# Sums by token behind further products in two attention layers, more rows ahead of the first logits, and a last bank in two halves

## The chip, the cores and the metric

The kernel runs on one core of a Trainium2 chip. The metric is the device time of one execution in microseconds (us). TensorE (PE) multiplies, VectorE (DVE), ScalarE (ACT) and GpSimd (POOL) do the elementwise work, SyncE (SP) issues the transfers; each of them works through its own list of instructions in order, and they wait for one another by semaphores. TensorE's results land in PSUM, which has eight banks of 512 float32 columns.

## The reference

Two decoder layers over 256 tokens of width 1024, in float32. Each layer is a half-step SwiGLU, a mixer, another half-step SwiGLU and a gated embedding. The mixer of layer 0 is latent attention (MLA), that of layer 1 forgetting attention (FoX). Cut to what matters here:

```python
def rms_norm(x, g):
    xf = x.astype(jnp.float32)
    y = xf * lax.rsqrt(jnp.mean(xf * xf, axis=-1, keepdims=True) + EPS)
    return (y * g.astype(jnp.float32)).astype(x.dtype)

def mla_mixer(hn, pos, w_in, g_q_lat, w_uq, g_kv_lat, w_ukv, g_qn, g_kn, w_o):
    z = hn @ w_in                                  # 512 + 256 + 32 columns
    c_q, c_kv, k_pe = ...
    q = (rms_norm(c_q, g_q_lat) @ w_uq).reshape(b, s, 16, 64 + 32)
    kv = (rms_norm(c_kv, g_kv_lat) @ w_ukv).reshape(b, s, 16, 64 + 64)
    k = jnp.concatenate([k_nope, k_pe_h], axis=-1)
    q, k = rms_norm(q, g_qn), rms_norm(k, g_kn)    # per head, then rope
    o = block_causal_attention(q, k, v)
    return o.reshape(b, s, 1024) @ w_o

def fox_mixer(hn, w_in, b_f, g_qn, g_kn, w_o):
    z = hn @ w_in                                  # q, k, v, and 16 forget logits
    log_f = jax.nn.log_sigmoid(f_logit)
    decay = jnp.cumsum(log_f, axis=1)
    o = block_causal_attention(rms_norm(q, g_qn), rms_norm(k, g_kn), v, decay)
    return o.reshape(b, s, 1024) @ w_o

    # the end of each layer
    gate = jax.nn.sigmoid(rms_norm(h, g_ple[i]) @ ple_w_gate[i])
    h = h + gate * (p[i] @ ple_w_proj[i])
```

## The kernel before

**Products.** Each float32 product is three passes in the rounded format float32r: high part by high part, low weight by high part, high weight by low part (L264 to L266 where the weights stream, `mm_x`; L234 to L236 where the tokens stream, `mm_w`). Weights come in units of up to 1 MB: SyncE loads a unit into one of three `raw` buffers (L70), ScalarE casts it to `whi` (L86), VectorE subtracts to get `wlo` (L87), each in pieces of up to 1024 columns; there are six `whi` and `wlo` buffers. Units are prefetched two ahead, at each `w.get()`. TensorE's results go to two PSUM tiles of two banks each, `pa`, and four of one bank, `pb`.

**Norms.** The RMS norms need sums of squares. ScalarE squares, GpSimd adds up chunks (`sq`, `ss` at L384 and L388; `zq` at L827 and L828), and TensorE sums over the partitions with a column of 1/1024, `mean_d`. `by_token` (L406) gives the mean square of each token with two matmuls of one column; `mean_squares` (L775) does the same for the latents of MLA. These sums are plain float32 matmuls.

**MLA.** `zmm(c)` multiplies by the 256 columns c of `w_in`; `latent(c)` turns them into the two parts of `zt` and their squares `zq`. Columns 2 and 3 are keys and rope, 0 and 1 queries. Then `keys(g)` (12 matmuls of 512 columns) and `queries(g)` (24 of 384) give keys, values and queries of four heads, g from 0 to 3. A head's norm for queries needs the token's mean square of the query latent, which is the sum over `zq` of columns 0 and 1: it stands at the end of `queries(0)`.

**Pairs.** Eight pairs of heads are worked on. `turn` transposes a pair's queries and keys (L612) into `qt` (copied by ScalarE, L616) and `kt` (VectorE, L614); `weigh` makes the logits (L518, L519), VectorE's maximum (L523), ScalarE's exponentials (L534), VectorE's division; `turn_back` transposes the weights (L547) into `pt` (one head by VectorE, one by ScalarE); `mix` multiplies by the values (L559, L564). In `mixed` (L710) the early parts, `keys` and `queries` 0 and 1 in MLA, run first; the late ones are fed between the steps of the pairs by a budget of rows, `each / 4` behind each step, with `each` 4 in MLA and 8 in FoX.

**FoX.** `group(272)` makes four heads of values and the forget logits, then `by_token` gives the norm. `dense(g)` (L1008) makes the queries, then the keys of four heads, each 48 matmuls of 256 columns; `more(g)` makes six heads of values.

**The end.** `ple_last` keeps tokens on the partitions: four products of half the depth by 512 output columns for two token tiles, 12 matmuls each, then a sigmoid from PSUM, a multiplication, an addition and a transfer for each 256 columns (L1134, L349, L1137).

**Order.** `steady`, `order` and `queue` are switches: while one is on, its instructions (matmuls; weight casts and subtractions; loads) keep the order of the program. What is not held may be placed by the scheduler.

Of the kernel before, what the change touches and what calls it, by code (L numbers as in the profile page):

```python
# [151 lines left out]
def trunk(ctx: ExitStack, tc: tile.TileContext, a: dict, out: bass.AP):  # L152
# [209 lines left out]
    class Norm:  # L362
# [38 lines left out]
        def by_token(self):  # L401
# [3 lines left out]
            for tt in range(2):  # L405
                nc.tensor.matmul(  # L406
                    ms[:, tt : tt + 1], lhsT=ss[:, tt * P : (tt + 1) * P], rhs=mean_d[:, 0:1], start=True, stop=True
                )
# [300 lines left out]
    def mixed(early, late, each, ready, pair, o, after):  # L709
# [8 lines left out]
        for j in range(-1, KD + 2):  # L718
# [8 lines left out]
            if 0 <= j < KD:  # L727
# [4 lines left out]
                rows.run(each / 4)  # L732
# [11 lines left out]
    def mla(norm, after, pool):  # L744
# [28 lines left out]
        def mean_squares(ps, zq):  # L773
            for tt in range(2):
                nc.tensor.matmul(  # L775
                    ps[:, tt : tt + 1], lhsT=zq[:, 0, tt * P : (tt + 1) * P], rhs=mean_d[:, :1], start=True, stop=True
                )
# [82 lines left out]
        def keys(g):  # L860
            wt = w.get()
# [24 lines left out]
            if g == 0:  # L886
                head_norms(ms, rk, 1, 2)
                norm_keys(g)

        def queries(g):  # L890
# [32 lines left out]
            got[g] = qn, kn, rk  # L923
            ready.add(g)

        def pair(j):
            qn, kn, rk = got[j // 2]
# [6 lines left out]
    def fox(norm, after, pool):  # L934
# [15 lines left out]

        v = pool.tile([P, 2, HEADS, VD], F32, name="v", tag="v", bufs=1)
# [56 lines left out]
        def dense(g):  # L1008

            ps = pa().rearrange("p (u t c) -> p u t c", u=2, t=2)  # L1010
            for u in range(2):
                wt = w.get()
                for k in range(KD):
                    for tt in range(2):
                        mm_x(ps[:, u, tt, :], wt(k), x, k, tt, start=(k == 0 and tt == 0), stop=(k == KD - 1))
                        yield 3 * PASS
# [267 lines left out]
```

## Time and profile before

| | us |
|---|---|
| median of three runs | 1048.11 |
| lowest, highest | 1047.37, 1049.19 |
| the profiled execution | 1049.13 |
| its span | 1047.4 |
| TensorE busy in it | 1034.1 (99%) |
| VectorE, ScalarE, GpSimd busy | 777.6, 600.0, 77.9 |

The profile is of one execution. A row of a timeline gives the start of an instruction, or of several alike in a row (x4), their time together, the engine, the line of the code, the tiles, and in brackets the engine's idle time before it with what ended it. TensorE's matmuls overlap, so a row's length is more than the distance to the next; the distance between starts is the pace. TensorE's clock was granted at 0.997 of full speed over the whole span.

### The profile page before, as it was taken

What the parts mean: (1) busy time and instruction counts of PE and PEld (TensorE: products, weight loads), DVE (VectorE), ACT (ScalarE), POOL (GpSimd) and SP (SyncE); (2) the same over time, 40 slices, a digit from 0 to 9 for tenths busy, and PEclk for the clock granted to TensorE, in tenths of its full rate; (3) what the DMA queues carried; (4) which work ended last, traced back from release to release, by engine and by line L of the source; (5) the groups of instructions that cost most, each with busy time, mean ns of one, the idle gap of its engine ahead of it and who ended that gap; (6) DMA issues with size and microseconds to landing.
All of it is one profiled execution on the core that took longest, in us unless ns stands there. A gap on an engine that the chain in (4) does not pass through costs nothing.

```text
span 1047.4 us, 16326 instructions
## 1 busy us (share of the span) xinstructions
PE 1034.1 (99%) x6380; PEld 918.5 (88%) x6380; DVE 777.6 (74%) x1369; ACT 600.0 (57%) x903; POOL 77.9 (7%) x99
## 2 busy tenths in 40 slices
PE   8999999999999999999999999999999999999998
PEld 7888888987898888889888888889998988888886
DVE  5888766679979776666987776658888797776664
ACT  6665544568766655455656555535655666554552
POOL 0000000233110000001110000011000200000010
PEclk9999999999999999999999999999999999999999
DMA  7765555524336656556537565554743267555541
GB/s 243 242 226 183 185 181 172 181 93 170 106 107 201 214 188 191 183 185 206 170 126 240 188 201 174 188 154 141 227 135 113 95 197 227 182 185 191 181 161 41
DMA packets 171105, 182.60 MB, mean 174 GB/s; under 512 B 6094, under 2 KB 164372, under 8 KB 171028
## 3 DMA queue, kind: packets, MB, share of 16 engines
q1 hardware_dynamic: 170452, 181.03, 53.7%
q8 instruction: 50, 0.82, 0.3%
q10 hardware_dynamic: 576, 0.53, 0.1%
q14 instruction: 27, 0.22, 0.1%
HBM read 180.50 MB, written 1.05 MB: 173 GB/s over the span
## 4 chain that ended last, share of the span: by engine, by line
PE 94%; DVE 3%; DMA 1%; POOL 1%; ACT 0%; issue 0%; ACTq 0%; DVEq 0%
PE pa L255 46%; PE pa L248 23%; PE pa L264 3%; PE pa L266 3%; PE pa L265 3%; PE pa L234 2%; PE pa L236 2%; PE pa L235 2%; DVE wlo L87 1%; PE pb L612 1%; PE pb L519 1%; PE pb L559 1%; PE pb L547 1%; PE pb L518 1%; DMA xn<-in_x_dram 1%; PE pb L266 1%
## 5 line engine op out<-in xcount | busy, mean ns | idle before, releaser
L87 DVE TENSOR_TENSOR wlo<-raw,whi 128x1024 fp32r<-128x1024 f32 (+2 forms) x351 | 418.5, 1223 | 170.9 <-PE pa L248 71.9
L86 ACT CAST whi<-raw 128x1024 fp32r<-128x1024 f32 (+2 forms) x351 | 351.0, 1016 | 247.0 <-PE pa L255 175.9
L255 PE MATMUL pa<-xa,whi 128*128 128x512 f32 x1408 | 343.9, 395 | 1.9 <-DVE xa L376 1.8
L255 PEld LDWEIGHTS pa<-xa,whi 128*128 128x128 f32 x1408 | 258.7, 189 | 54.1 <-DVE xa L376 3.1
L248 PEld LDWEIGHTS pa<-xa,wlo 128*128 128x128 f32 x1408 | 179.1, 189 | 8.7
L248 PE MATMUL pa<-xa,wlo 128*128 128x256 f32 x1408 | 180.6, 279 | 0.0
L255 PE MATMUL pa<-hid,whi 128*128 128x512 f32 x704 | 169.2, 392 | 0.0
L255 PEld LDWEIGHTS pa<-hid,whi 128*128 128x128 f32 x704 | 128.8, 188 | 25.2
L384 POOL TENSOR_TENSOR sq<-sq 128x512 f32<-128x512 f32 x21 | 37.8, 1800 | 826.9 <-ACT sq L382 813.4
L248 PEld LDWEIGHTS pa<-hid,wlo 128*128 128x128 f32 x704 | 88.3, 188 | 4.0
L248 PE MATMUL pa<-hid,wlo 128*128 128x256 f32 x704 | 89.1, 278 | 0.0
L264 PE MATMUL pa<-whi,xa 128*128 128x256 f32 (+3 forms) x192 | 59.0, 307 | 0.0
L266 PE MATMUL pa<-whi,xa 128*128 128x256 f32 (+3 forms) x192 | 57.6, 300 | 0.0
L265 PE MATMUL pa<-wlo,xa 128*128 128x256 f32 (+3 forms) x192 | 57.2, 298 | 0.0
L234 PE MATMUL pa<-xa,whi 128*128 128x256 f32 x184 | 54.2, 295 | 0.0
L349 DVE TENSOR_TENSOR hid<-hf,hid 128x512 fp32r<-128x512 f32 x44 | 30.4, 692 | 29.0 <-ACT hid L442 29.0
L236 PE MATMUL pa<-xa,wlo 128*128 128x256 f32 x184 | 51.9, 283 | 0.0
L235 PE MATMUL pa<-xa,whi 128*128 128x256 f32 x184 | 51.9, 282 | 0.0
L432 ACT COPY gt<-pa 128x512 f32<-128x512 f32 x44 | 25.8, 586 | 39.1 <-PE pa L248 39.0
L432 ACT COPY hf<-pa 128x512 f32<-128x512 f32 x44 | 25.7, 584 | 28.1 <-PE pa L248 28.1
L438 ACT ACTIVATE gt<-gt 128x512 f32<-128x512 f32 x44 | 27.7, 629 | 19.4 <-DVE gt L349 19.3
L264 PEld LDWEIGHTS pa<-whi,xa 128*128 128x128 f32 x192 | 36.1, 188 | 1.4 <-issue 0.5
(281 smaller groups left out, 1215.1 us busy)
## 6 DMA issues: line engine op xcount, KB each, us to landing
raw<-in_ffn_w_in_dram SPq DMA_DIRECT2D x86, 1024.0 KB, 5.1
raw<-in_ffn_w_out_dram SPq DMA_DIRECT2D x32, 1024.0 KB, 5.2
raw<-in_ffn_w_out_dram SPq DMA_DIRECT2D x16, 768.0 KB, 4.5
raw<-in_ple_w_gate_dram SPq DMA_DIRECT2D x8, 1024.0 KB, 5.8
raw<-in_fox_w_in_dram SPq DMA_DIRECT2D x8, 1024.0 KB, 6.5
raw<-in_mla_w_o_dram SPq DMA_DIRECT2D x4, 1024.0 KB, 5.6
raw<-in_fox_w_o_dram SPq DMA_DIRECT2D x4, 1024.0 KB
raw<-in_mla_w_in_dram SPq DMA_DIRECT2D x3, 1024.0 KB, 6.7
```

Source lines behind the costliest of these rows:

```text
L86: self.order(self.nc.scalar.copy(h, whole))
L87: self.order(self.nc.vector.tensor_tensor(low, whole, h.bitcast(F32), op=ALU.subtract))
L234: steady(nc.tensor.matmul(ps, lhsT=hi, rhs=x[:, k, 0, :], start=start, stop=False, skip_group_check=True))
L235: steady(nc.tensor.matmul(ps, lhsT=hi, rhs=x[:, k, 1, :], start=False, stop=False, skip_group_check=True))
L236: return steady(nc.tensor.matmul(ps, lhsT=lo, rhs=x[:, k, 0, :], start=False, stop=stop, skip_group_check=True))
L248: nc.tensor.matmul(ps[:, 1, :], lhsT=wt(k)[1][:, cols], rhs=x[:, at + k, 0, :], start=False, stop=(k == last), skip_group_check=True,)
L255: nc.tensor.matmul(ps, lhsT=wt(k)[0][:, cols], rhs=x[:, at + k], start=(k == first), stop=False, skip_group_check=True)
L264: steady(nc.tensor.matmul(ps, lhsT=x[:, k, 0, t], rhs=wt[0], start=start, stop=False, skip_group_check=True))
L265: steady(nc.tensor.matmul(ps, lhsT=x[:, k, 0, t], rhs=wt[1], start=False, stop=False, skip_group_check=True))
L266: steady(nc.tensor.matmul(ps, lhsT=x[:, k, 1, t], rhs=wt[0], start=False, stop=stop, skip_group_check=True))
L384: nc.gpsimd.tensor_tensor(sq, sq, self.acc, op=ALU.add)
L432: nc.scalar.copy(o, ps[:, :, 0, :])
```

## The change

**MLA.** `steady` is on from `keys(0)` to the sums for the queries, and `mean_squares` is held by it. The sums move from the end of `queries(0)` to the end of `keys(1)` (`first_queries`), with the norms of the first queries. `zmm(1)` then stands ahead of `keys(0)`, where it stood behind.

**Rows ahead of the first logits.** Behind `turn` of pair 0 `mixed` spends `each` instead of a quarter: three units more in MLA, six in FoX.

**FoX.** `dense(0)` is begun early: its first half, the 48 matmuls of the queries, is issued ahead of `by_token`, which is held there by `steady`.

**End.** In the last 512 output columns the second token tile is two PSUM banks of 256 columns, finished one after the other, in place of one of 512.

```diff
@@ by_token
-                nc.tensor.matmul(
-                    ms[:, tt : tt + 1], lhsT=ss[:, tt * P : (tt + 1) * P], rhs=mean_d[:, 0:1], start=True, stop=True
+                steady(
+                    nc.tensor.matmul(
+                        ms[:, tt : tt + 1], lhsT=ss[:, tt * P : (tt + 1) * P], rhs=mean_d[:, 0:1], start=True, stop=True
+                    )
                 )
@@ mixed
                 pairs.append(pair(j))
                 pairs[j].turn()
-                rows.run(each / 4)
+                rows.run(each / 4 if j else each)
@@ mla (mean_squares is wrapped in steady in the same way)
         def keys(g):
+            if g == 0:
+                steady.on = True
             wt = w.get()
...
             if g == 0:
                 head_norms(ms, rk, 1, 2)
                 norm_keys(g)
+            elif g == 1:
+                first_queries()
+
+        def query_norms(g):
+            kn, ms, rk = got[g][1:4] if g == 0 else got[g]
+            nc.vector.scalar_tensor_tensor(ms[:, 0], ms[:, 0], 1.0 / QK, by_head(yq), op0=ALU.mult, op1=ALU.add)
+            head_norms(ms, rk, 0, 1 if g == 0 else 2)
+
+        def first_queries():
+
+            sq = pb()
+            mean_squares(sq, sqa)
+            steady.on = False
+            nc.vector.scalar_tensor_tensor(yq, sq[:, :2], D / QR, ex, op0=ALU.mult, op1=ALU.add)
+            nc.vector.tensor_scalar(yq, yq, EPS, None, op0=ALU.mult)
+            query_norms(0)
 
         def queries(g):
...
-            if g == 0:
-                sq = pb()
-                mean_squares(sq, sqa)
-                nc.vector.scalar_tensor_tensor(yq, sq[:, :2], D / QR, ex, op0=ALU.mult, op1=ALU.add)
-                nc.vector.tensor_scalar(yq, yq, EPS, None, op0=ALU.mult)
...
-            nc.vector.scalar_tensor_tensor(ms[:, 0], ms[:, 0], 1.0 / QK, by_head(yq), op0=ALU.mult, op1=ALU.add)
-            if g == 0:
-                head_norms(ms, rk, 0, 1)
-            else:
-                head_norms(ms, rk, 0, 2)
+            if g:
+                query_norms(g)
                 norm_keys(g)
@@ fox
-        order.on = True
-        order.on = True
+        order.on = steady.on = True
         Rows(group(272)).all()
         vf = got.pop("ps")
+        zero = dense(0)
+        for _ in range(2 * KD):
+            next(zero)
         xt = norm.by_token()
+        steady.on = False
...
-        mixed([dense(0), more(0), dense(1)], [more(1), dense(2), dense(3)], 8, lambda g: len(got.get(g, ())) == 2, pair, o, after)
+        mixed([zero, more(0), dense(1)], [more(1), dense(2), dense(3)], 8, lambda g: len(got.get(g, ())) == 2, pair, o, after)
@@ ple_last
-        gp = [[both_t[:, tt] for tt in range(2)], [pb() for tt in range(2)]]
+
+        gp = [[(0, both_t[:, 0], 0, 512), (1, both_t[:, 1], 0, 512)], None]
         for kh in range(2):
             for half in range(2):
                 wt = w.get()
-                c = slice(half * 512, (half + 1) * 512)
-                for tt in range(2):
+                if gp[half] is None:
+                    gp[half] = [(tt, pb()[:, : c1 - c0], c0, c1) for tt, c0, c1 in ((0, 0, 512), (1, 0, 256), (1, 256, 512))]
+                for tt, ps, c0, c1 in gp[half]:
                     for k in range(4):
-                        mm_x(gp[half][tt], wt(k), x, kh * 4 + k, tt, start=(kh + k == 0), stop=(kh == 1 and k == 3))
+                        part_of = tuple(z[:, c0:c1] for z in wt(k))
+                        mm_x(ps, part_of, x, kh * 4 + k, tt, start=(kh + k == 0), stop=(kh == 1 and k == 3))
...
-                for tt in range(2):
-                    for q in range(2):
-                        cq = slice(q * 256, (q + 1) * 256)
-                        co = slice(half * 512 + q * 256, half * 512 + q * 256 + 256)
+                for tt, ps, c0, c1 in gp[half]:
+                    for cq in range(0, c1 - c0, 256):
+                        co = slice(half * 512 + c0 + cq, half * 512 + c0 + cq + 256)
...
-                        nc.scalar.activation(gt, gp[half][tt][:, cq], AF.Sigmoid, scale=r[:, tt : tt + 1])
+                        nc.scalar.activation(gt, ps[:, cq : cq + 256], AF.Sigmoid, scale=r[:, tt : tt + 1])
```

How the instructions stand is shown at three places. The rows give the line, the operation, out<-in with the tiles' numbers, and the shape; lines below the first edit have moved up by a few numbers in the code after.

TensorE in MLA, before, around the sums for the queries; `zq_2093` is what GpSimd adds up, the matmuls above them are the last of `queries(0)`, those below the first of `keys(1)`:

```order
L264 MATMUL pa_2262<-whi_2145,zt_1933 128x384
L265 MATMUL pa_2262<-wlo_2146,zt_1933 128x384
L266 MATMUL pa_2262<-whi_2145,zt_1933 128x384
L775 MATMUL pb_2288<-mean_d_118,zq_2093 128x1 x2
L264 MATMUL pa_2321<-whi_2209,zt_1933 128x512
L265 MATMUL pa_2321<-wlo_2210,zt_1933 128x512
L266 MATMUL pa_2321<-whi_2209,zt_1933 128x512
```

The same sums after:

```order
L264 MATMUL pa_2304<-whi_2209,zt_1933 128x512
L265 MATMUL pa_2304<-wlo_2210,zt_1933 128x512
L266 MATMUL pa_2304<-whi_2209,zt_1933 128x512
L778 MATMUL pb_2328<-mean_d_118,zq_2093 128x1 x2
L264 MATMUL pa_2355<-whi_2254,zt_1933 128x384
L265 MATMUL pa_2355<-wlo_2255,zt_1933 128x384
L266 MATMUL pa_2355<-whi_2254,zt_1933 128x384
```

They now have `keys(1)` above and `queries(1)` below them; 48 matmuls of `zmm(1)` that stood between `keys(0)` and `queries(0)` stand ahead of both.

ScalarE in MLA, before, from the casts of the last `uq` unit (`raw_2345`) to the first cast of `w_o` (`raw_2421`), with the exponentials of pair 0 (`sm_2437`, `sm_2450`) and `qt_2466` of pair 1 between:

```order
L86 CAST whi_2493<-raw_2345 128x768
L86 CAST whi_2497<-raw_2345 128x768
L872 ACTIVATE scr_2483<-pa_2427 128x512
L534 ACT_TABLE_LOAD
L534 ACTIVATE sm_2437,mx_2438<-sm_2437,mx_2438,rk_2228 128x128
L534 ACTIVATE sm_2437,mx_2438<-sm_2437,mx_2438,rk_2228 128x256
L534 ACTIVATE sm_2450,mx_2451<-sm_2450,mx_2451,rk_2228 128x128
L534 ACTIVATE sm_2450,mx_2451<-sm_2450,mx_2451,rk_2228 128x256
L616 ACTIVATE qt_2466<-pb_2467,qsc_298 96x512
L878 COPY kn_2480<-pa_2427 128x8x64
L880 ACTIVATE v_2205<-pa_2427,rs_2117 128x256 x2
L86 CAST whi_2614<-raw_2421 128x1024
```

The same stretch after, up to the first two exponentials of pair 0 (`sm_2474`); `raw_2421` is `w_o` again, and `qt_2503` is that of pair 1:

```order
L86 CAST whi_2453<-raw_2345 128x768
L86 CAST whi_2457<-raw_2345 128x768
L878 ACTIVATE scr_2443<-pa_2427 128x512
L86 CAST whi_2581<-raw_2421 128x1024
L618 ACTIVATE qt_2503<-pb_2504,qsc_298 96x512
L884 COPY kn_2440<-pa_2427 128x8x64
L886 ACTIVATE v_2205<-pa_2427,rs_2117 128x256 x2
L536 ACT_TABLE_LOAD
L536 ACTIVATE sm_2474,mx_2475<-sm_2474,mx_2475,rk_2228 128x128
L536 ACTIVATE sm_2474,mx_2475<-sm_2474,mx_2475,rk_2228 128x256
```

The first cast of `w_o` has moved from behind the exponentials of pair 0 to ahead of `qt` of pair 1, and `kn` and `v` of the third group stand ahead of the exponentials.

TensorE at the start of FoX, before, around the sums by token; `ss_6940` is GpSimd's sum, the matmuls above are the last of `group(272)`, those below the first of `dense(0)`:

```order
L264 MATMUL pa_6948<-whi_6900,xa_5326 128x272
L265 MATMUL pa_6948<-wlo_6901,xa_5326 128x272
L266 MATMUL pa_6948<-whi_6900,xa_5326 128x272
L406 MATMUL pb_7017<-mean_d_118,ss_6940 128x1 x2
L264 MATMUL pa_7067<-whi_6951,xa_5326 128x256
L265 MATMUL pa_7067<-wlo_6952,xa_5326 128x256
L266 MATMUL pa_7067<-whi_6951,xa_5326 128x256
```

After:

```order
L264 MATMUL pa_7017<-whi_6955,xa_5326 128x256
L265 MATMUL pa_7017<-wlo_6956,xa_5326 128x256
L266 MATMUL pa_7017<-whi_6955,xa_5326 128x256
L407 MATMUL pb_7076<-mean_d_118,ss_6940 128x1 x2
L264 MATMUL pa_7017<-whi_6985,xa_5326 128x256
L265 MATMUL pa_7017<-wlo_6986,xa_5326 128x256
L266 MATMUL pa_7017<-whi_6985,xa_5326 128x256
```

The sums now stand between the two halves of `dense(0)`, behind the queries (`whi_6955` is the second piece of their weights) and ahead of the keys (`whi_6985`).

At the end of the program the last 12 matmuls are of 256 columns, as the 12 before them, into another bank.

## Rows read from the trace of the kernel before

**Rows 1.** The page, part 1: engine, busy us (share of the span), number of instructions
```profile
PE 1034.1 (99%) x6380; PEld 918.5 (88%) x6380; DVE 777.6 (74%) x1369; ACT 600.0 (57%) x903; POOL 77.9 (7%) x99
```

**Rows 2.** Timeline of TensorE, MLA layer: start us, length us, engine, line, out<-in, [idle <-releaser]
```profile
213.08 0.28 PE L234 MATMUL pa<-xa,whi 128*128 128x256 f32 x1
...
218.74 0.35 PE L264 MATMUL pa<-whi,zt 128*128 128x384 f32 x1
...
220.49 0.45 PE L264 MATMUL pa<-whi,zt 128*128 128x384 f32 x1
...
223.20 0.34 PE L266 MATMUL pa<-whi,zt 128*128 128x384 f32 x1
224.67 0.61 PE L775 MATMUL pb<-mean_d,zq 128*128 128x1 f32 x4 [1.14 <-POOL zq L828]
```

**Rows 3.** Timeline of all engines at the start of the FoX layer
```profile
709.91 5.43 DVE L87 TENSOR_TENSOR wlo<-raw,whi 128x1024 fp32r<-128x1024 f32 x4 [0.97 <-ACT whi L86]
...
710.40 1.59 POOL L388 TENSOR_TENSOR ss<-sq 128x256 f32<-128x256 f32 x1
...
710.60 0.28 PE L266 MATMUL pa<-whi,xa 128*128 128x272 f32 x1
...
712.04 0.61 PE L406 MATMUL pb<-mean_d,ss 128*128 128x1 f32 x4 [1.16 <-POOL ss L388]
```

**Rows 4.** Timeline of VectorE at the end of the program
```profile
1042.83 1.46 DVE L349 TENSOR_TENSOR gn<-gn,xa 128x256 f32<-128x256 f32 x4 [1.34 <-ACT gn L1134]
```

**Rows 5.** Windows: stretch, its us, busy us of each engine (instructions), clock, DMA
```profile
222.50:250.00 27.50, 25.49 (x142) 21.14 (x142) 26.76 (x79) 22.32 (x45) 11.75 (x13) 1.00 0.57 192
```

**Rows 6.** Timeline of TensorE, MLA layer, first logits and transposes
```profile
232.17 0.60 PE L612 MATMUL pb<-ident,qn 128*96 128x128 f32 x4
232.61 0.60 PE L612 MATMUL pb<-ident,kn 128*96 128x128 f32 x4
...
243.06 0.49 PE L518 MATMUL pb<-kt,qt 96*128 96x128 f32 x2 [0.59 <-ACT qt L616]
...
244.47 1.02 PE L547 MATMUL pb<-ident,sm 128*128 128x128 f32 x6
245.70 0.61 PE L612 MATMUL pb<-ident,qn 128*96 128x128 f32 x4 [0.20 <-DVE mx L523]
```

**Rows 7.** Timeline of ScalarE, MLA layer
```profile
220.99 0.60 ACT L770 ACTIVATE zq<-pa 128x512 f32<-128x512 f32 x1 [0.55 <-DVE zt L766]
...
236.82 1.57 ACT L86 CAST whi<-raw 128x768 fp32r<-128x768 f32 x2 [2.37 <-DMA raw<-in_mla_w_uq_dram]
...
238.90 1.28 ACT L534 ACT_TABLE_LOAD   x1
...
242.34 0.67 ACT L616 ACTIVATE qt<-pb,qsc 96x512 f32<-96x512 f32 x1
...
244.09 1.04 ACT L86 CAST whi<-raw 128x1024 fp32r<-128x1024 f32 x1
```

**Rows 8.** Timeline of GpSimd, MLA layer
```profile
221.66 1.29 POOL L827 TENSOR_TENSOR zq<-zq 128x512 f32<-128x512 f32 x1 [2.41 <-ACT zq L770]
223.03 1.59 POOL L828 TENSOR_TENSOR zq<-zq 128x256 f32<-128x256 f32 x1
```

**Rows 9.** Timeline of VectorE, MLA layer
```profile
235.30 1.21 DVE L87 TENSOR_TENSOR wlo<-raw,whi 128x1024 fp32r<-128x1024 f32 x1
...
238.83 0.95 DVE L87 TENSOR_TENSOR wlo<-raw,whi 128x768 fp32r<-128x768 f32 x1
...
239.86 0.68 DVE L614 COPY kt<-pb 96x512 f32<-96x512 f32 x1
...
240.54 0.67 DVE L875 TENSOR_REDUCE msq<-scr 128x8 f32<-128x512 f32 x1
```

**Rows 10.** Timeline of the DMA issues on SyncE, MLA layer
```profile
233.94 8.65 SPq L70 DMA_DIRECT2D raw<-in_mla_w_o_dram  x3
```

**Rows 11.** The page, part 6: DMA issues, count, KB each, median us to landing
```profile
raw<-in_mla_w_o_dram SPq DMA_DIRECT2D x4, 1024.0 KB, 5.6
```

More of the change, by code (lines that the diff above doesn't have):

```diff
@@ L774, in mean_squares @@
             for tt in range(2):
-                nc.tensor.matmul(
-                    ps[:, tt : tt + 1], lhsT=zq[:, 0, tt * P : (tt + 1) * P], rhs=mean_d[:, :1], start=True, stop=True
+                steady(
+                    nc.tensor.matmul(
+                        ps[:, tt : tt + 1], lhsT=zq[:, 0, tt * P : (tt + 1) * P], rhs=mean_d[:, :1], start=True, stop=True
+                    )
                 )
@@ L916, in queries @@
             pool_op(qn[:, :, :, NOPE:], ra, rb, ALU.add)
[L917 to L921 removed]
+            if g:
+                query_norms(g)
                 norm_keys(g)
[L923 removed]
+            got[g] = qn, kn, ms, rk
             ready.add(g)
         def pair(j):
[L927 removed]
+            qn, kn, _, rk = got[j // 2]
             hs = slice(2 * (j % 2), 2 * (j % 2) + 2)
@@ L949, in group, with dense @@
             got["ps"] = ps
+        def dense(g):
+            ps = pa().rearrange("p (u t c) -> p u t c", u=2, t=2)
+            for u in range(2):
+                wt = w.get()
+                for k in range(KD):
+                    for tt in range(2):
+                        mm_x(ps[:, u, tt, :], wt(k), x, k, tt, start=(k == 0 and tt == 0), stop=(k == KD - 1))
+                        yield 3 * PASS
+            ms = pool.tile([P, 2, 2, 4], F32, name="fms", tag="fms")
+            rk = pool.tile([P, 2, 2, 4], F32, name="frk", tag="frk")
+            for u in range(2):
+                scr = pool.tile([P, 512], F32, name="scr", tag="scr", bufs=2)
+                nc.scalar.activation(scr.rearrange("p (t c) -> p t c", t=2), ps[:, u], AF.Square)
+                nc.vector.tensor_reduce(
+                    ms[:, u].rearrange("p t h -> p (t h)"), scr.rearrange("p (h c) -> p h c", c=HD), axis=AX.X, op=ALU.add
+                )
+            nc.vector.scalar_tensor_tensor(ms, ms, 1.0 / HD, exb, op0=ALU.mult, op1=ALU.add)
+            rsqrt(ms.rearrange("p u t h -> p (u t h)"), 16, rk.rearrange("p u t h -> p (u t h)"))
+            got[g] = []
+            for u in range(2):
+                t4 = pool.tile([P, 2, 4, AUG], F32, name="qk"[u] + "a", tag="qk"[u] + "a")
+                tt_op(
+                    t4[:, :, :, :HD], ps[:, u].rearrange("p t (h c) -> p t h c", h=4),
+                    rk[:, u].unsqueeze(3).broadcast_to([P, 2, 4, HD]), ALU.mult,
+                )
+                nc.gpsimd.memset(t4[:, :, :, HD + 1 - u], 1.0)
+                got[g].append(t4)
+            if g:
+                decay(g)
         v = pool.tile([P, 2, HEADS, VD], F32, name="v", tag="v", bufs=1)
         o = act.tile([P, KD, 2, S], F32R, name="xa", tag="xa")
-        order.on = True
-        order.on = True
+        order.on = steady.on = True
         Rows(group(272)).all()
         vf = got.pop("ps")
+        zero = dense(0)
+        for _ in range(2 * KD):
+            next(zero)
         xt = norm.by_token()
+        steady.on = False
         r = pool.tile([P, 2], F32, name="fr", tag="fr", bufs=1)
```

29 lines of the change are left out of this document (removed).

## The prediction

> **What bounds the kernel now.** I read the page first: TensorE is busy 1034.1 us of a span of 1047.4 us [rows 1], so a gain comes out of some 13 us in which it idles, or out of the two ends. Then the table of TensorE's waits, whose larger entries lead to the timelines around them. In the MLA layer the last matmul of `queries(0)` begins at 223.20 and the sums of squares of the query latent (L775) only at 224.67, since GpSimd's `zq` is late [rows 2]; less one matmul's pace of 0.17 us, 1.30 us are lost. In the FoX layer the last 272-column product begins at 710.60 and the sums by token (L406) at 712.04, behind GpSimd's `ss` [rows 3]; less 0.13 us of pace, 1.31 us. Last the end of the program: after TensorE's last matmul and a sigmoid, VectorE does four steps in 1.46 us before the last output can leave [rows 4].
>
> Behind the MLA wait another limit stands close. From 222.5 to 250.0 us VectorE is busy 26.76 of 27.50 us [rows 5], and TensorE waits for what comes from it and from ScalarE: 0.59 us at the logits of pair 1, and in the six transposes of the weights of pair 0, which take from 244.47 to 245.70, 1.23 us, where four others take 0.44 us, so that six should take 0.66 [rows 6]. The question of this case is whether TensorE's earlier start there is kept.
>
> **The change part by part.**
>
> *FoX.* GpSimd's second add ends at 711.99 (710.40 and 1.59), and the sums follow at once [rows 3]. With 48 products of 256 columns ahead of them (5.6 us: `zmm(1)` is 48 of these, from 213.08 to 218.74, 0.118 us each, [rows 2]), `ss` is ready long before its matmul; the wait is gone. What is late next: the second of these products multiplies by `wlo`, and VectorE's first `wlo` there begins at 709.91. Four take 5.43 us [rows 3]; I give the first 1.5 us, so it is there at 711.4, where TensorE would want it at 710.84. So 0.6 us of a new wait stand against 1.31 us: **0.7 us** gained. The chain to the square root begins later than now: two `wlo` of 768 columns more stand ahead of it on VectorE, 0.95 us each [rows 9], and ScalarE empties the values' PSUM buffer some 1.9 us later. That buffer is wanted back only after both halves of `dense(0)`, 96 matmuls or 11.3 us behind 711.4, so at 723, and the chain to its release ends about 721: nothing. If that cover were gone, it would cost at most those 1.9 us.
>
> *Tail.* Now VectorE's four steps of 1.46 us all stand behind the last matmul, since the last bank of 512 columns is finished by it [rows 4]. With two banks of 256 columns, the first half's sigmoid and two steps run under the second bank's 12 matmuls (1.4 us by the pace above). One sigmoid and two steps stay behind the end: two steps of 0.365 us fewer, 0.73 us, less a few hundredths for twice as many matmuls. **0.7 us.** The bounds are narrow, 0.4 to 0.8: it would be less if the first half's two steps were still at work when the last sigmoid ends.
>
> *MLA, the front.* Now `zmm(1)` runs before `keys(0)`, and the sums stand behind `keys(1)`. `zmm(1)` ends 2.86 us earlier, near 215.9, so ScalarE's `zq` begins near 218.1 instead of 220.99 [rows 7], and GpSimd's two adds of 1.29 and 1.59 us end near 221.7 instead of 224.62 [rows 8]. Their matmul is reached near 225.7. The 1.30 us are gone with 4 us to spare. So are small delays in `queries(0)`, which begins now right behind `zmm(1)` and catches up with `zt`: the matmul at 220.49, whose row is 0.45 long instead of 0.34 [rows 2], and its two neighbours start 0.39 us late in all. Together 1.7 us: `queries(1)` ends near 230.4 instead of 232.1.
>
> *MLA, what takes it back.* VectorE does not get less to do; the norms of `keys(0)`, which it did before 219 while nobody pressed, now fall into the full stretch. Its order puts a second `wlo` of 768 columns (0.95 us) and a reduction (0.67 us) ahead of the copy `kt` of pair 1, which stands at 239.86 for 0.68 us now [rows 9]: 239.86 + 0.95 + 0.67 + 0.68 = 242.2. On ScalarE the first cast of `w_o` moves ahead of `qt` of pair 1 and waits for its DMA. Its issue, at 233.94 [rows 10], hangs on the buffer of the second `uq` unit and comes at about 234.5; the median landing is 5.6 us [rows 11], so 240.1; the cast takes 1.04 us and `qt` 0.67 us [rows 7]: 241.8. So logits 1 starts near 242.2, by `kt`; now it is 243.06 [rows 6]. The products done by then are the same but one (24 matmuls of `queries(2)`, now 23). Without a wait TensorE would be there at 243.06 − 0.59 − 1.7 = 240.8: of 1.7 us **0.86** are left. Next the exponentials of pair 0: `qt`, `kn` and `v` (1.75 us, from 242.34 to 244.09), then the table load and the exponentials (3.44 us, from 238.90 to 242.34, [rows 7]) stand behind the `w_o` cast, so they end near 246.4. TensorE reaches the transposes near 245.5, after logits (1.4 us) and eight products of 512 columns (1.9 us), and they wait about 0.9 us there, where 0.57 us are lost now. That takes 0.3 us. I take **0.6 us** for the MLA layer. Its bounds are −0.7 us (a further wait of 1.3 us at the first `mix`: four `w_o` casts of 1.04 us then stand in a row ahead of `pt` on ScalarE, two of them behind TensorE's last use of their buffers) and +1.7 us (nothing given back).
>
> A rule of the Trainium skill bears on this. ScalarE stood idle 2.37 us before the casts at 236.82, which waited for a transfer [rows 7]. The Trainium skill, "TensorE: Matmul & The Clock Gate", section "Architectural detail: the array is 16× 32×32, not 1× 128×128", says that ScalarE's and VectorE's queues are strictly first in, first out, which speaks against a cast put ahead of `qt`. The trace agrees with its 2.37 us. If ScalarE could pass, the wait at the transposes would go and the sum would be 2.9 us instead of 2.0.
>
> A second: VectorE's four `wlo` at 709.91 took 1.36 us each, the first two beside GpSimd's adds [rows 3], and 1.21 us alone [rows 9]: stretched, not stopped. The Trainium skill, "SBUF — State Buffer", section "Who interferes with whom", says that a VectorE instruction with two SBUF inputs and a GpSimd one that reads SBUF lock each other out for a whole instruction. By that rule a `wlo` ahead of `kt` could lose a GpSimd add of 1.3 us more and the sum would be 0.7 us; the trace differs, and I go by it.
>
> *Sum.* 0.7 + 0.7 + 0.6 = **2.0 us**. The profiled execution took 1049.13 us, so 1047.1 us; the median of the runs shown, 1048.11 us, lies 1.02 us lower, so **1046.1 us**. About 0.2% (2.1 us) is what a measurement of this kernel can tell from no change, so the forecast stands on that edge.
>
> **The rivals.**
>
> A. *MLA gains nothing.* VectorE sets the pace from 222 to 250, and whatever TensorE gains at 224 it waits for later. For: 26.76 of 27.50 us busy [rows 5]. Against: at logits 1 it is ScalarE's `qt`, not VectorE, that comes last now [rows 6]. Gain 0.7 + 0.7: 1046.7 us.
>
> B. *All is kept.* The rows pulled ahead of the first logits (3 more units in MLA, 6 in FoX) cover the later waits too: 1.7 us in front, 0.59 at logits 1, 0.57 at the transposes, with FoX and the tail 4.3 us: 1043.8 us. For: TensorE has work of its own ready there. Against: the additions for `kt` and `qt` above.
>
> C. *Slower.* The first `w_o` cast stands on ScalarE ahead of `qt` of pair 1 and of all exponentials. If its transfer lands late, the softmax waits for a weight that nobody needs yet, and after 0.4 us of slack each us costs one. Where it lands 2.4 us later than I take it, 8 us after its issue, the 2.0 us are used up; after 10 us the time is 1050.1 us. For: three transfers of 1 MB are issued in 8.65 us [rows 10]. Against: the median of 5.6 us [rows 11].
>
> D. *The FoX part only changes the wait's name.* The first `wlo` ends 0.7 us later than I take it, and 1.31 us are waited for as now: 1046.8 us.
>
> **How the numbers follow.** Forecast 0.45 (gains of 1.4 to 2.8 us); A 0.22; B 0.18; C 0.08; D 0.07. Faster by over 0.2%: somewhat over half of the forecast, and B, 0.43. Slower by over 0.2%: C, 0.08. The rest, 0.49, lies within. The range for 8 in 10 leaves out C and the far half of B, and reaches beyond A by 0.8 us for the lower MLA bound: 1043.9 to 1047.5 us.
>
> **What would show it.** In the profile after: the sums in FoX no longer wait for `ss`, nor those of the queries for `zq`; in their place 0.6 us of the first `dense` product for `wlo` at 711; at logits 1 a wait of about 1.4 us for `kt` or `qt`, until 242.2; on ScalarE a `w_o` cast that waits for its DMA near 240; behind the last matmul two VectorE steps. I am wrong on MLA if logits 1 begins after 243.1 (A) or before 241 (B), on FoX if the wait at 711 is over 1 us, and on the tail if four steps still follow the last matmul.

## The result and the profile after

On the same chip the kernel after takes 1056.31 us (median of four runs, 1053.64 to 1056.67), the kernel before 1047.85 us. The ratio is 1.0073, with a 95% interval of 1.0054 to 1.0092: slower by 0.7%, where 1046.1 us, a small gain, was forecast, and beyond the range that ended at 1047.5. The profiled execution took 1056.32 us with a span of 1054.6 us; before it was 1049.13 and 1047.4.

First the page, part 1 (engine, busy us, share, instructions), which answers to [rows 1]:

```profile
PE 1036.1 (98%) x6404; PEld 920.5 (87%) x6404; DVE 781.0 (74%) x1369; ACT 600.5 (57%) x903; POOL 79.0 (7%) x99
```

TensorE is busy 2.0 us longer with the same products (24 of the last ones are cut in two), and idles 5.2 us more. Where, the stretches between fixed points of TensorE's timeline tell. "MLA front" runs from the sums by token (L406, now L407) to the first transposes of pair 0's queries, "MLA pairs" from there to the sums of squares of the norm behind the mixer; "FoX start" from the first 272-column product to the cumulative sum of the forget logits, "FoX pairs" from there to the next norm; "end" from the first product of the last gated embedding's second input (tile `pt_in`) to the end of the span. Each number is a difference of two starts in the trace, in us:

| kernel | MLA front | MLA pairs | FoX start | FoX pairs | end | span |
|---|---|---|---|---|---|---|
| before | 23.06 | 84.00 | 27.29 | 107.20 | 35.41 | 1047.4 |
| after | 25.73 | 88.83 | 26.62 | 108.68 | 34.87 | 1054.6 |
| difference | +2.67 | +4.83 | −0.67 | +1.48 | −0.54 | +7.2 |

What is left, −0.57 us, lies in the start of the program and the feed-forward parts, which the change doesn't touch; their sum differs by up to 3.1 us between any two profiles here.

**MLA front.** TensorE's timeline, which answers to [rows 2]:

```profile
208.14 0.50 PE L407 MATMUL pb<-mean_d,ss 128*128 128x1 f32 x4
208.50 0.58 PE L778 MATMUL pb<-mean_d,zq 128*128 128x1 f32 x4
209.01 0.30 PE L797 MATMUL pb<-ident,kpet 32*128 32x32 f32 x2
211.75 0.39 PE L234 MATMUL pa<-xa,whi 128*128 128x256 f32 x1 [2.43 <-ACT zq L772]
...
214.90 0.41 PE L236 MATMUL pa<-xa,wlo 128*128 128x256 f32 x1
215.12 0.41 PE L234 MATMUL pa<-xa,whi 128*128 128x256 f32 x1
...
228.74 0.39 PE L266 MATMUL pa<-whi,zt 128*128 128x512 f32 x1
228.97 0.50 PE L778 MATMUL pb<-mean_d,zq 128*128 128x1 f32 x4
```

The sums over the queries' `zq` now follow their neighbour with no wait, as intended: the row at 228.97 has no bracket. But `zmm(1)`, which now comes first, waits 2.43 us for a `zq` on ScalarE. The rows of ScalarE show which:

```profile
210.07 0.47 ACT L767 ACTIVATE zt<-pa,gvec 128x256 fp32r<-128x256 f32 x1 [1.26 <-DVE zt L768]
211.10 0.60 ACT L772 ACTIVATE zq<-pa 128x512 f32<-128x512 f32 x1 [0.55 <-DVE zt L768]
```

These are the steps of `latent(0)`, the columns just finished. Its `zq` is the last reader of a PSUM tile of two banks; `zmm(0)` has written the first, `zmm(1)` writes the second. Before, the same `zq` was done at 212.67, while TensorE still had `keys(0)` to do, and `zmm(1)` began at 213.08 [rows 2] without a wait:

```profile
212.07 0.60 ACT L770 ACTIVATE zq<-pa 128x512 f32<-128x512 f32 x1 [0.55 <-DVE zt L766]
```

```profile
212.85 0.39 PE L266 MATMUL pa<-whi,zt 128*128 128x512 f32 x1
```

Back in the kernel after: when TensorE starts again, its matmuls stand 0.21 us apart (214.90, 215.12) where they take 0.118 [rows 2]. A window (us, busy us of PE, PEld, DVE, ACT, POOL with instructions, granted clock, DMA) says why:

```profile
212.60:215.80 3.20, 3.20 (x18) 3.20 (x17) 0.97 (x8) 0.00 (x0) 0.00 (x0) 0.50 0.02 5
```

The granted clock is 0.50, the lower level of 1.2 GHz: 15 matmuls, 1.4 us more.

**MLA pairs.** TensorE at the first two logits, the transposes of pair 0's weights and the first output product, to set beside [rows 6]:

```profile
240.02 0.46 PE L520 MATMUL pb<-kt,qt 96*128 96x128 f32 x2 [0.73 <-DVE msq L900]
...
246.20 0.46 PE L520 MATMUL pb<-kt,qt 96*128 96x128 f32 x2 [1.13 <-DVE mx L531]
...
250.08 0.33 PE L549 MATMUL pb<-ident,sm 128*128 128x128 f32 x1 [0.48 <-DVE sm L541]
...
264.49 0.39 PE L234 MATMUL pa<-xa,whi 128*128 128x256 f32 x1 [1.35 <-ACT v L886]
```

Four waits of 3.69 us, where [rows 6] has two of 0.79 us. The first output product waits for `v` of the last keys, since ScalarE empties that buffer late. ScalarE in the same stretch, to set beside [rows 7], and SyncE's issue of `w_o`, beside [rows 10]:

```profile
243.71 1.05 ACT L86 CAST whi<-raw 128x1024 fp32r<-128x1024 f32 x1 [3.31 <-DMA raw<-in_mla_w_o_dram]
244.67 0.67 ACT L618 ACTIVATE qt<-pb,qsc 96x512 f32<-96x512 f32 x1
...
247.87 0.49 ACT L536 ACTIVATE sm<-sm,mx,rk 128x128 f32<-128x128 f32 x1
```

```profile
238.44 5.76 SPq L70 DMA_DIRECT2D raw<-in_mla_w_o_dram  x3
```

The `w_o` cast ahead of `qt` does wait for its transfer, 3.31 us, which is how rival C would begin. VectorE is as full as in [rows 5]:

```profile
224.20:251.70 27.50, 25.16 (x141) 22.16 (x140) 26.64 (x88) 20.56 (x40) 12.29 (x13) 1.00 0.58 192
```

**FoX start.** The rows that answer to [rows 3]:

```profile
717.17 0.29 PE L266 MATMUL pa<-whi,xa 128*128 128x272 f32 x1
717.29 0.28 PE L264 MATMUL pa<-whi,xa 128*128 128x256 f32 x1
718.03 0.39 PE L265 MATMUL pa<-wlo,xa 128*128 128x256 f32 x1 [0.46 <-DVE wlo L87]
...
723.37 0.28 PE L266 MATMUL pa<-whi,xa 128*128 128x256 f32 x1
723.49 0.50 PE L407 MATMUL pb<-mean_d,ss 128*128 128x1 f32 x4
```

The sums at 723.49 no longer wait for `ss`; the first product by `wlo` waits instead, 0.74 us from start to start less 0.12 of pace, 0.62 us.

**End.** VectorE behind the last matmul, beside the four steps of 1.46 us in [rows 4]:

```profile
1050.44 1.10 DVE L349 TENSOR_TENSOR gn<-gn,xa 128x256 f32<-128x256 f32 x3 [0.93 <-ACT gn L1153]
```

Three steps stand there, not two: one that belongs ahead of the last sigmoid was left behind it.

### The profile page after: what moved, and what is told of

The parts are those of the page before. It is cut to its first block, busy times and chain, and to the rows that moved or that the text cites. A ratio compares the mean times of both kernels' runs of the same rounds, so it can differ in the third digit from the quotient of the medians.

```text
span 1054.6 us, 16374 instructions
## 1 busy us (share of the span) xinstructions
PE 1036.1 (98%) x6404; PEld 920.5 (87%) x6404; DVE 781.0 (74%) x1369; ACT 600.5 (57%) x903; POOL 79.0 (7%) x99
## 4 chain that ended last, share of the span: by engine, by line
PE 92%; DVE 6%; DMA 1%; ACT 1%; issue 0%; POOL 0%; ACTq 0%; DVEq 0%
PE pa L255 46%; PE pa L248 23%; PE pa L264 2%; PE pa L234 2%; PE pa L265 2%; PE pa L266 2%; PE pa L236 2%; PE pa L235 2%; DVE wlo L87 2%; PE pb L614 1%; PE pb L561 1%; PE pb L521 1%; PE pb L549 1%; DMA xn<-in_x_dram 1%; PE pb L264 1%; PE pb L266 1%
## 5 line engine op out<-in xcount | busy, mean ns | idle before, releaser
L255 PEld LDWEIGHTS pa<-xa,whi 128*128 128x128 f32 x1408 | 258.4, 189 | 54.1 <-DVE xa L376 3.1
L234 PEld LDWEIGHTS pa<-xa,whi 128*128 128x128 f32 x184 | 35.3, 192 | 6.5 <-ACT zq L772 2.5
```

The source lines that it names most:

```text
L234: steady(nc.tensor.matmul(ps, lhsT=hi, rhs=x[:, k, 0, :], start=start, stop=False, skip_group_check=True))
L255: nc.tensor.matmul(ps, lhsT=wt(k)[0][:, cols], rhs=x[:, at + k], start=(k == first), stop=False, skip_group_check=True)
```

## The experiments

Each run is told with its ratio to the kernel before and the stretch that its edit touches. Diffs are against the kernel after unless another is named, and cut to their main lines ("..."). "Pulled rows" are the units of late products that the change puts ahead of the first logits; they have nothing to do with rows of the profile.

**e1, two PSUM tiles for the query latents.** `zmm(0)` and `zmm(1)` each get a tile of one bank.

```diff
-        zps = [pa().rearrange("p (b t) -> p b t", b=4) for _ in range(2)]
+        zp1 = pa().rearrange("p (b t) -> p b t", b=4)
+        zpb = {}
+
+        def zview(c):
+            if c >= 2:
+                return zp1[:, 2 * (c % 2) : 2 * (c % 2) + 2, :]
+            if c not in zpb:
+                zpb[c] = pb().rearrange("p (b t) -> p b t", b=2)
+            return zpb[c]
...
```

> The kernel after, with the columns 0 and the columns 1 of the latent product in two PSUM tiles of one bank each, in place of one tile of two banks. The order of the instructions stays. Theory 1 (the loss is two separate things: zmm(1) waits 2.4 us for zq since both latents lie in one tile, and then runs 3.2 us at half clock, together 4.2 us; and the rows pulled ahead of the first logits cost the rest): the wait at zmm(1) and the half clock are gone, the MLA layer is about 4 us shorter, the time about 1052. Theory 2 (one thing: everything later is late only because of that wait): about 1048 or less. Rival (the wait is for something else than the tile): the wait stays, about 1056.

Measured: 1051.85 us, 1.0039 (1.0024 to 1.0054). TensorE's timeline and the clock in the stretch that ran at 0.50:

```profile
209.26 0.30 PE L805 MATMUL pb<-ident,kpet 32*128 32x32 f32 x2
209.50 0.38 PE L234 MATMUL pb<-xa,whi 128*128 128x256 f32 x1
```

```profile
212.50:215.70 3.20, 3.20 (x27) 3.11 (x27) 1.27 (x10) 0.46 (x1) 0.00 (x0) 1.00 0.00 0
```

No wait and the full clock: the MLA front is 21.50 us, 4.23 less than after and 1.56 less than before. So the 2.43 us and the half clock have one cause, the shared tile, and without it the front gains nearly what was forecast, 1.56 of 1.7 us. The Trainium skill, "PSUM — Partial Sum Buffer", section "PSUM bank collisions raise a hardware error", has two engines at work on different banks without a collision; e1's rows agree: `zmm(1)` begins at 209.50 and runs on while ScalarE reads the other latent's bank for `zq` at 211.35. So the wait in after came from how the tile is tracked, not from a need of the banks. The MLA pairs stay at 88.85 us (88.83): what is lost there doesn't depend on the front.

**e2, `keys(0)` ahead of `zmm(1)` again.** `steady` goes on in `queries(0)` in place of `keys(0)`.

```diff
         def keys(g):
-            if g == 0:
-                steady.on = True
...
         def queries(g):
+            if g == 0:
+                steady.on = True
```

> The kernel after, with keys(0) ahead of zmm(1) again as before, all else as after (sums behind keys(1), more rows ahead of the first logits). keys(0) covers latent(0). Theory 1: no wait for zq at zmm(1), no half clock, MLA about 4 us shorter, about 1052, like the split tiles. Theory 2: about 1048 or less. If the sums' move itself costs (VectorE's or ScalarE's full stretch), it stays above 1054.

Measured: 1049.88 us, 1.0024 (1.0013 to 1.0035); front 22.25, pairs 87.15 us. The old cover is back and with it 3.48 us of the front. The pairs gain 1.68 us too, more than the 0.75 us of front that e1 has over e2: `zmm(1)` first costs more behind than it brings.

**e3, no more rows ahead of the first logits**, in both layers.

```diff
-                rows.run(each / 4 if j else each)
+                rows.run(each / 4)
```

> The kernel after, with a quarter of the rows ahead of the first logits in both layers as before; the wait of zmm(1) stays. Theory 1: the w_o cast is behind the exponentials of pair 0 again, MLA from the first transposes on is about 5 us shorter and FoX behind its sums about 1.5 us, so about 1050; the wait of 2.4 us and the half clock are still there. Theory 2: little changes, about 1055.

Measured: 1052.70 us, 1.0047 (1.0030 to 1.0064). MLA pairs 85.71 us, 3.12 less than after; FoX pairs 107.32 us, 1.36 less. The front keeps its 25.73 us. By these stretches the pulled rows, costed at nothing, cost 4.48 us, about as much as the wait in the front with its clock, 4.23 us (e1).

**e4, e2 and e3 together.**

> Both: keys(0) ahead of zmm(1), and a quarter of the rows ahead of the first logits in both layers. What is left of the change is the sums' move in MLA, the early dense half in FoX, and the last columns in two banks. Theory 1: both costs are gone and what was forecast for the three remaining parts shows, 0.7 us each for FoX and the tail and 0.6 to 1.7 for MLA: 1045.0 to 1046.2. If the sums' move gives nothing (rival A of the prediction), 1046.7; if VectorE's full stretch makes it worse, above 1047.5.

Measured: 1046.21 us, 0.9988 (0.9978 to 0.9998). Front 22.25 (−0.81 against before), pairs 84.48 (+0.48), FoX start 26.62 (−0.67), FoX pairs 107.31 (+0.11), end 34.85 (−0.56). This is the best version found, 0.12% under before, which is less than 0.2%.

**e5, the `w_o` casts held behind the exponentials of pairs 0 and 1**, on top of e2.

```diff
+                order.on = j in (1, 2) and each == 4
                 pairs[j - 1].weigh()
...
-                    nc.scalar.activation(
+                    order(
+                        nc.scalar.activation(
...
+                    )
```

> As e2 (keys(0) first, more rows ahead of the first logits), but the exponentials of pairs 0 and 1 and the weight casts are kept in the order of the program there, so that the casts of w_o stand behind these exponentials on ScalarE, and no longer ahead of qt of pair 1. Theory: it is the cast waiting for its transfer ahead of qt, kn, v and the exponentials that makes the stretch from the first transposes to the end of MLA 2.7 us longer in e2 than in e4; then it falls from 87.15 to about 84.5 to 85 us and the time to about 1047.5 (the more rows in FoX stay). Rival: it is the pulled rows themselves, by VectorE's full stretch; then it stays near 87 us and the time near 1049.9.

Measured: 1054.13 us, 1.0061 (1.0045 to 1.0078); pairs 90.54 us, 3.39 more than e2. TensorE's three largest waits there:

```profile
257.17 0.55 PE L551 MATMUL pb<-ident,sm 128*128 128x128 f32 x3 [1.58 <-DVE xa L349]
...
261.21 0.39 PE L234 MATMUL pa<-xa,whi 128*128 128x256 f32 x1 [0.91 <-ACT v L887]
...
264.53 0.43 PE L563 MATMUL pb<-pt,v 128*64 128x256 f32 x1 [1.64 <-ACT pt L554]
```

ScalarE shows why. It stands idle for 6.05 us until VectorE has the next maxima, with `kn` and `v` behind, and two casts of `w_o` stand ahead of `pt`:

```profile
258.79 0.49 ACT L537 ACTIVATE sm<-sm,mx,rk 128x128 f32<-128x128 f32 x1 [6.05 <-DVE mx L531]
...
261.05 1.99 ACT L86 CAST whi<-raw 128x1024 fp32r<-128x1024 f32 x2
```

So holding the casts back gains nothing. Since the hold brings a wait of its own, it doesn't tell what the cast ahead of `qt`, rival C's mechanism, costs; e11 does.

**e6, e1 and e3 together**, and **e7, e1 with the casts of e5** and no more rows in FoX.

> As e4 (a quarter of the rows ahead of the first logits), but with zmm(1) ahead of keys(0) as in the kernel after and the two latents in two PSUM tiles (e1). The front of MLA is 0.75 us shorter than in e4 (21.50 against 22.25 us). If TensorE keeps it: 1045.5. If the stretch behind is set by VectorE (rival A of the prediction), the stretch from the first transposes on grows by as much and the time is that of e4, 1046.2.

> More rows ahead of the first logits in MLA alone, with two PSUM tiles for the latents and the w_o casts held behind the exponentials of pairs 0 and 1. If the cast was the only cost of the pulled rows, it is as good as e6 or better by the waits that the rows cover, 1045 to 1045.5; if the pulled rows cost by themselves, 1046.5 to 1048.

Measured: e6 1047.68 us, 0.9999 (0.9990 to 1.0008), front 21.48, pairs 85.72 us. e7 1053.47 us, 1.0058 (1.0044 to 1.0071), front 21.71, pairs 92.37 us. e7 repeats e5's verdict, with 6.12 us idle on ScalarE and, from 259.80 to 263.20, the clock at 0.50; that is up to 1.7 us of its pairs (an estimate, half of these 3.40 us). e6 against e4 sets the two orders side by side without the pulled rows: `zmm(1)` first has a front 0.77 us shorter and pairs 1.24 us longer. TensorE at the first logits, in e6 and then in e4:

```profile
236.02 0.46 PE L520 MATMUL pb<-kt,qt 96*128 96x128 f32 x2 [2.15 <-DVE msq L908]
```

```profile
235.29 0.46 PE L520 MATMUL pb<-kt,qt 96*128 96x128 f32 x2 [1.19 <-DVE kt L616]
```

Both wait for VectorE, e6 0.96 us longer. e3, with the wait in front, has pairs of 85.71 us, the same as e6's 85.72: their length follows from the order behind the front, not from how early TensorE arrives there.

**e8, the FoX start and the end alone**: `mla` is that of before (these lines are left out), and there are no more rows.

```diff
-                rows.run(each / 4 if j else each)
+                rows.run(each / 4)
```

> The kernel before with only the early dense half in FoX and the last columns in two banks; MLA and the rows ahead of the logits as before. The stages of e4 give 0.67 us for FoX and 0.56 us for the tail: 1046.3 against 1047.55 of before. Against e4 it tells what the move of the sums in MLA is worth by itself: 0.3 us by the stages.

Measured: 1046.43 us, 0.9992 (0.9983 to 1.0001). There is no profile of it to read by stretches, only its times: 0.22 us from e4. Moving the MLA sums brings next to nothing even with the old cover.

**e9 and e10, the pulled rows alone**, in MLA and in FoX, everything else as before (diff against before; in both, the sums by token are also wrapped in `steady` as in after, which changes nothing there: e10's FoX start takes 27.28 us, before's 27.29).

```diff
-                rows.run(each / 4)
+                rows.run(each if j == 0 and each == 4 else each / 4)
```

```diff
-                rows.run(each / 4)
+                rows.run(each if j == 0 and each == 8 else each / 4)
```

> The kernel before with one edit: three units more of rows behind the first turn in MLA; the sums, zmm(1), FoX and the end are as before. Theory P (the pulled rows cost by themselves, whatever the sums do): the stretch of MLA from the first transposes to the query-free end of the layer's mixer grows from 84.0 us to 86.5 to 87.2, the whole by 2.5 to 3.1 us, 1.0024 to 1.0030. Rival I (they only cost together with the moved sums, whose norms then fall into the same stretch): the stretch stays at 84.0 within 0.5, the ratio within 0.9995 to 1.0005.

> The kernel before with one edit: six units more of rows behind the first turn in FoX. Theory P: FoX from the sums to the last mix grows from 107.2 us to 108.5 or 108.7, the whole by 1.3 to 1.5 us, 1.0012 to 1.0014. Rival I: it stays at 107.2 within 0.3, the whole within 0.3 us.

Measured: e9 1053.59 us, 1.0054 (1.0037 to 1.0071), MLA pairs 89.80 us, 5.80 more than before. e10 1048.93 us, 1.0014 (1.0004 to 1.0024), FoX pairs 108.60 us, 1.40 more. Rival I falls in both layers; theory P holds in FoX in size, and in MLA the cost is twice what it said. Up to 1.7 us of that is the clock (an estimate, half of the 3.50 us at about half speed below); the rest, 4.1 us, is still more than its 3.2. TensorE in e9, at the second logits and the first output product, and the clock behind that:

```profile
242.52 0.46 PE L520 MATMUL pb<-kt,qt 96*128 96x128 f32 x2 [2.27 <-DVE ks L349]
...
261.08 0.39 PE L234 MATMUL pa<-xa,whi 128*128 128x256 f32 x1 [1.40 <-ACT v L882]
```

```profile
261.50:265.00 3.50, 3.50 (x17) 2.60 (x15) 3.17 (x7) 1.53 (x5) 1.16 (x2) 0.51 0.04 11
```

**e11, one unit more in place of three**, on top of e2, without more rows in FoX.

```diff
-                rows.run(each / 4 if j else each)
+                rows.run(each / 4 if j else (each / 2 if each == 4 else each / 4))
```

> keys(0) ahead of zmm(1) as in e2, no more rows in FoX, and one unit more of rows in MLA in place of three. Theory G (each unit pulled forward costs its share): the stretch of MLA behind the first transposes lies a third of the way from 84.48 us (none) to 87.15 us (three), near 85.4. Rival T (a step: it costs once the first w_o casts pass the exponentials, and nothing ahead of that): 84.5 within 0.3, or 87 within 0.4.

Measured: 1050.37 us, 1.0025 (1.0015 to 1.0035); pairs 87.38 us, as with three units (87.15). A step, then: the first unit costs 2.90 us against e4, and theory G falls. TensorE at the second logits, where e4 doesn't wait:

```profile
242.52 0.46 PE L520 MATMUL pb<-kt,qt 96*128 96x128 f32 x2 [1.54 <-DVE rs_t L357]
```

But the step has not the condition that rival T gave it. In e11 the first `w_o` cast stands behind `qt` and the exponentials of pair 0, and doesn't wait; in e2 it stands ahead of them and waits. First ScalarE in e11, then in e2:

```profile
237.44 0.69 ACT L618 ACTIVATE qt<-pb,qsc 96x512 f32<-96x512 f32 x1 [0.86 <-PE pb L614]
...
239.44 0.50 ACT L536 ACTIVATE sm<-sm,mx,rk 128x128 f32<-128x128 f32 x1
...
242.88 1.04 ACT L86 CAST whi<-raw 128x1024 fp32r<-128x1024 f32 x1
```

```profile
237.76 1.05 ACT L86 CAST whi<-raw 128x1024 fp32r<-128x1024 f32 x1 [2.64 <-DMA raw<-in_mla_w_o_dram]
238.72 0.68 ACT L618 ACTIVATE qt<-pb,qsc 96x512 f32<-96x512 f32 x1
```

The pairs are equally long with and without a cast ahead of `qt`, so rival C's mechanism isn't needed for their length.

**e12, `kn` and `v` of the last keys held ahead of the `w_o` casts**, on top of e2.

```diff
+            order.on = g == 3
-            nc.scalar.copy(kn[:, :, :, :NOPE], kv4[:, :, :, :NOPE])
+            order(nc.scalar.copy(kn[:, :, :, :NOPE], kv4[:, :, :, :NOPE]))
...
```

> keys(0) ahead of zmm(1) as in e2, all rows, and ScalarE's kn and v of the last keys held ahead of its w_o casts, so that their PSUM buffer comes free for the first output products. The scheduler then also puts some products ahead of the first logits. Theory V (that buffer is the largest single loss behind the pulled rows, 1.4 of 2.7 us): the stretch behind the first transposes falls from 87.15 us to 85.5 to 86.0. Rival M (no single wait: what is moved comes back elsewhere, as when the casts were held behind the exponentials): 87.15 or more.

Measured: 1051.05 us, 1.0035 (1.0015 to 1.0056); pairs 88.12 us, 0.97 more than e2. The output product waits no more, and two other waits are there:

```profile
242.33 0.50 PE L264 MATMUL pa<-whi,zt 128*128 128x512 f32 x1 [2.45 <-ACT v L886]
...
261.61 0.49 PE L520 MATMUL pb<-kt,qt 96*128 96x128 f32 x2 [1.52 <-ACT qt L618]
```

Theory V falls: that wait is gone, others stand in its place, and TensorE's idle time in the pairs is 4.57 us, where e2 has 3.22.

**What the rows do.** The products are the same in number in every kernel; they are only dealt out differently. The table counts them by their pace (0.228 us for 512 columns, 0.1745 for 384), in us of TensorE:

| kernel | ahead of the first logits | between the first and second logits | MLA pairs |
|---|---|---|---|
| before | 1.37 | 5.38 | 84.00 |
| e4 | 1.37 | 5.38 | 84.48 |
| e6 | 2.91 | 1.22 | 85.72 |
| e2 | 4.31 | 3.30 | 87.15 |
| e11 | 2.74 | 3.66 | 87.38 |
| e12 | 4.31 | 4.90 | 88.12 |
| after | 4.31 | 2.62 | 88.83 |
| e9 | 4.31 | 2.27 | 89.80 |

Before, the first logits begin at 234.66 us, 0.2 us after the pace of the products ahead would have them, so more products put there cover nothing. Between the first and second logits, where the chain of maxima, exponentials, `kt` and `qt` goes on, they are then missing: the waits at the second logits are 2.27 us in e9, 1.54 in e11 and 1.13 after, 0.59 before, none in e4. That is the smaller part of the loss, though. Counted from the first transposes, the second logits come after 12.33 us and 6.93 us of products in the kernel after, and after 10.89 us and 6.75 us before: 1.3 us lost of 4.83. In e11 (11.22 us and 6.40 us) and e2 (12.29 and 7.61) they are within 0.3 us of e4 (11.35 and 6.75). So most of the loss, and in e11 and e2 nearly all of it, arises behind the second logits.

Nor is all of it idle time of TensorE. The windows of the whole pairs (us, busy us of PE and the others), in before, after, e4 and e11:

```profile
232.17:316.17 84.00, 83.10 (x565) 70.89 (x564) 73.53 (x232) 60.70 (x135) 22.61 (x22) 1.00 0.40 132
```

```profile
233.87:322.70 88.83, 84.09 (x564) 71.17 (x564) 77.60 (x244) 61.64 (x135) 21.88 (x22) 1.00 0.38 125
```

```profile
231.68:316.16 84.48, 82.90 (x566) 71.06 (x564) 73.91 (x234) 61.24 (x135) 23.05 (x22) 1.00 0.39 130
```

```profile
231.30:318.68 87.38, 85.40 (x566) 71.30 (x564) 73.46 (x234) 60.89 (x135) 24.16 (x22) 1.00 0.38 125
```

Of after's 4.83 us 3.84 are idle time (4.74 us against 0.90), of e11's 2.90 us only 0.40 (1.98 against 1.58). The rest lies in longer distances from one matmul to the next, without a wait in the rows.

That every kernel of the table with more than 1.37 us ahead of the first logits has longer pairs is shown. e6 is one of them though it has no pulled rows: with `zmm(1)` first, the scheduler itself puts 2.91 us there. Neither column orders these kernels among themselves (e12 has nearly all of its cover, e6 least), and e5, e7 and e12 each removed one suspected wait and met another. So which of the engines' steps sets the length of the pairs once the rows are moved stays open; so does some 1.9 us of after's 4.83 that no wait listed above names (4.83 less 3.69 − 0.79 = 2.90), 0.97 us of it in three smaller waits of its trace and about 1 us in none.

## Why the prediction was wrong

The sum was 2.0 us gained; by the stretches, 7.8 us were lost. In its order:

- **FoX start: right.** 0.7 us forecast, 0.67 measured; the new wait of 0.6 us for `wlo` is 0.62. Rival D falls.
- **End: right, a little too large.** 0.7 us forecast, 0.54 measured, within 0.4 to 0.8. The text took two of VectorE's four steps off the end; one went, since its order has one step of the first half behind the last sigmoid.
- **MLA front: the step that failed first.** "`zmm(1)` ends 2.86 us earlier, near 215.9" took the sums of the tokens to be the last thing ahead of it. The wait for the last reader of its PSUM tile was not looked for, because before `keys(0)` stood in between and the wait had no row: 2.8 us of keys were its cover. A moved step was checked against its operands, not against the tile that it writes. Then the clock added to it. e1 shows both: without the shared tile the front gains 1.56 us, where 1.7 was forecast, so the rest of the step was sound.
- **What the MLA takes back: right as far as it went, and this step failed too.** Counted from the first transposes, the text has the weights' transposes 16.0 us behind (246.4 less 230.4); measured are 16.21, where [rows 6] has 12.30. Its cast of `w_o` that waits ahead of `qt` is in the rows. But there the account ended: 3.7 us later, with 2.9 us of rows done ahead of time, was read as 0.3 us lost, as if those rows came back as slack behind. The bound of −0.7 us priced one more wait. Measured are +4.83 us, which the runs divide: +0.48 for the moved sums (e4 against before), +1.23 for `zmm(1)` first (e3 against e4; both without pulled rows), +3.12 for the rows (after against e3).
- **FoX pairs: not in the sum.** Six units more were named under rival B as cover and given no price. They cost 1.36 (e3) to 1.40 us (e10).
- **The rivals.** B was wrong in sign: the rows that were to cover later waits made them. C gives 1050.1 us and the right side, and its wait is there, 3.31 us; but e11's pairs are as long as e2's without it, and e5 and e7 gain nothing by taking it away. That C is on the right side is luck. A, with no gain from MLA, has its premise borne out (VectorE full, 26.64 of 27.50 us), and e4 and e8 agree within 0.22 us as it would have it, but it saw no loss.
- **A reading that was wrong.** The prediction took VectorE's four subtractions at 709.91 to last 1.36 us each, stretched by GpSimd and not stopped, and so set aside a rule by which the two engines lock each other out. One by one they last 1.49, 1.74, 1.21 and 1.21 us, and the first two are stopped: each ends 1.08 us behind the end of the GpSimd instruction that was running when it began (710.32, and 711.99 by [rows 3]). Nor was the one at 235.30 alone, since GpSimd worked from 234.90 to 236.83. The rows of both engines, in order of time:

```profile
709.02 1.30 POOL L384 TENSOR_TENSOR sq<-sq 128x512 f32<-128x512 f32 x1 [4.13 <-ACT sq L382]
709.91 1.49 DVE L87 TENSOR_TENSOR wlo<-raw,whi 128x1024 fp32r<-128x1024 f32 x1 [0.97 <-ACT whi L86]
...
711.33 1.74 DVE L87 TENSOR_TENSOR wlo<-raw,whi 128x1024 fp32r<-128x1024 f32 x1
```

  It doesn't explain the loss: in the MLA pairs 21 subtractions take 26.5 us in all after, and 27.1 in e4, the best version.

## What to carry to other kernels

When an instruction moves, look up the last reader of every buffer that it writes, also where the old order showed no wait: what stood in between may have been the cover. Work that is pulled ahead is taken from somewhere; find the wait that it covers now and the one that it covered before, and where it covers none now, leave it. Carry the account of a shifted chain on to the end of its stage, and time edits one by one: of these four, two gained 1.2 us together, and the others lost it several times over.

## What the runs showed of the hardware

TensorE's clock fell to 0.50 in the middle of a kernel that keeps TensorE busy 98% of its span, and not always behind the longest waits. In the kernel after it fell behind the 2.43 us wait at 211.75, ahead of which the engine had only one-column sums and two 32-column transposes from 208.14 on; in e9 behind the 1.40 us wait at 261.08, ahead of which it had transposes and two matmuls of a mix; in e7 behind the 1.65 us wait at 258.58. In all three it was back at 1.00 within some 5 us. It did not fall behind 2.45 us in e12 (at 242.33, the window to 245.30 at 1.00), 2.15 us in e6 (at 236.02) or 1.64 us in e5 (at 264.53). One place shows both: in a feed-forward part that no edit touches TensorE waits for `xa`, in the kernel before 1.84 us at 521.98, and there the clock falls in eleven of the profiles. The window in the kernel before:

```profile
522.20:525.60 3.40, 3.40 (x13) 3.01 (x13) 1.78 (x3) 2.02 (x4) 1.31 (x2) 0.50 0.87 278
```

In e10 and e5 the same wait takes 1.83 and 1.84 us, and the clock stays; e10 from its wait at 520.98 on:

```profile
521.20:524.60 3.40, 3.40 (x22) 3.01 (x22) 3.22 (x5) 2.03 (x4) 1.31 (x2) 1.00 0.85 277
```

So the length of a wait alone doesn't tell what it costs, nor does its place: 13 matmuls were done in the first stretch, 22 in the second.

A weight subtraction on VectorE can be stopped by a GpSimd instruction, as the two at 709.91 and 711.33 above are. In the kernel before 22 subtractions last over 1.3 us, and 19 of these end 1.08 or 1.09 us behind the end of a GpSimd instruction that was running when they began. Not every one is stopped: the one at 235.30 lasts 1.21 us, though a GpSimd instruction runs from 234.90 to 236.83.
